# A hybrid encoder layer in fp32: moving weight splits, residual loads, token operands and one POOL subtraction

## The chip, the cores and the metric

The kernel runs on one core of a Trainium2 chip, in one launch. The metric is device time in microseconds, the median of several runs; lower is better. The engines are named as in the profile: PE (TensorE, matmuls), PEld (its weight loads), DVE (VectorE), ACT (ScalarE), POOL (GpSimd) and SP (SyncE, here a queue of DMAs).

## The reference

One encoder layer over two sequences, 2048 tokens (sample) and 256 tokens (prompt), with 1024 channels and shared weights:

```
p = rmsnorm(x) @ W_in                       # 2336 columns
a = bidirectional gated linear attention    # 4 heads, 512 channels, chunks of 64
b = spatial gating over chunks of 128       # 256 channels
c = centred mean pooling, windows 2/4/8/16  # 256 channels
x = x + concat(a, b, c) @ W_o
h = rmsnorm(x)
gate, up = split(h @ W1)                    # 2 x 2816 columns
x = x + (silu(conv3(gate)) * up) @ W2       # depthwise conv of width 3 over tokens
y = rmsnorm(x)
```

All is in fp32. Each large product is made of three fp32r matmuls: both operands are split into a high and a low part (hi = the rounded copy, lo = source - hi), and hi*hi + hi*lo + lo*hi is added up in PSUM.

## The kernel before, in words

**Splits and ticks.** `split` (L159) makes the high part on ACT (L161 or, with a scale, L164) and the low part on DVE or POOL (L162, L165). `mm3` (L168) is the three matmuls. Small work that goes along with the matmuls is written as Python generators in a `Pipe` (L91): after each group of three matmuls the program calls `tick`, and every generator that is due issues its next step; what it yields is the number of ticks to its next one. From the second tile of the second sweep on, DVE, ACT, POOL and SP execute in just the order in which the program issues their work (`manual_schedule`, L854); PE does so everywhere. Before that the framework's planner orders DVE, ACT, POOL and SP by its own estimate of when each instruction can start.

**First sweep** (L189 to L494). 18 token tiles of 128. The first 1312 columns of W_in are split once into eight tiles wk; each token tile is multiplied by them (`main1`), 24 ticks a tile, and `post1` does the attention inside the chunks. Masked copies go into buffers af and ab and the low-rank gate into lrs, two of each (NZ). From tile 12 on the raw second weights, wb, are loaded into the ring rawt of four buffers, which `wo_prep` used before. The last tile runs with k outermost, so that the wk tiles come free one after the other; its evictions and its post1 (`end1`) are issued in the second sweep.

**Second sweep** (L497 to L876). The other 1024 columns, wb, are split into eight tiles vk. These lie where wk lay. Three `w2prep(k)` are issued ahead of the first tile's matmuls, the others between them; each asks for the raw tile four further on as it ends. `main2` makes gates and spatial gating, `out2` multiplies by W_o for a group of tiles (SUPERS), adds x, stores the sum to DRAM (d_x) and adds up squares; `stat2` turns these into the norm's factors with a matmul over ones. The last `out2` runs while the FFN's first operands are made (L1360).

**FFN** (L886 to L1405). Three blocks of 2 x 384 tokens (the last with the prompt). h @ W1 is done by Strassen's scheme in its seven-product form: per FFN tile j (22 of them, 128 gate and 128 up columns each) seven products of 4 ticks each, in this order, with token operands in brackets: A11 (B11), S1 (T1), S2 (T2), S3 (T3), S4 (B22), A12 (B21), A22 (T4); 28 ticks in all (`ffn1`). The products go into five PSUM banks fA to fE; A12 adds to fA and A22 to fD, so fD must have been read by `u3` (L1202) first.

The weight operands are made one step a product by `operands` (L1081), four of them ahead in fa. In block 0 each j loads A11, A12, A21, A22 (rawop), makes S1 to S4 on POOL (`comb`, L1072) and stores them to DRAM; the later blocks load all seven. Low halves of A are on DVE, of S on POOL (L1079). The token operands lie in four tiles B0 to B3 by pairs p (B0: B11, B21; B1: T3, B22; B2: T1, T2; B3: T4, half as wide), of one buffer each. For blocks 1 and 2 `bmake` writes them unsplit to DRAM and `bload` (L1031), started with the last FFN tile of the block before, loads and splits the sixteen pieces (four k by four p), with the low halves of p = 0 and 2 on DVE and of p = 1 and 3 on POOL (PAIRS).

After the products of a j, `gate` (L1172) runs twice, for each half of the tokens: conv and SiLU between ACT and DVE, then a split into uh and ul. `ffn2` (L1251) multiplies by W2 after each part of 2 or 3 tiles (PARTS; the FFN always runs one tile ahead) and adds into x2, the residual, loaded by `load2f` (L1275) from d_x. With a block's last part, `sqadd` takes squares on ACT (L1242) and adds them on POOL (L1244), `finish` (L1283) makes the norm's factor, scales x2, stores y and loads the next block's x2. At the very end `last_norm` (L1320) does the same for group 0, with the chain cut short.

The order of SP's queue around the change: at the end of the second sweep the stores of out2, the four transfers of x2 (L924, two for each half), then the stores and loads of `operands` (L1070, L1065).

Of the kernel before, what the change touches and what calls it, by code (L numbers as in the profile page):

```python
# [18 lines left out]
P = 128  # L19
# [21 lines left out]
HW1 = 656  # L41
EV = 0
TX = (4, 0, 3, 1)
# [8 lines left out]
HP = (5, 3, 3, 3)  # L52
HL = (1, 2)
BM = (12, 9, 1, 6, 3)
# [65 lines left out]
def trunk(ctx: ExitStack, tc: tile.TileContext, xT, wa, wb, gw2, gb, rows, wsT, plw, wo, w1, w2, vec, cst, yT):  # L120
# [66 lines left out]
    msk = swp.tile([P, 2, P], U8, name="msk")  # L187
    xpool = pool("xpool", 2)
    if True:  # L189
        w1p = pool("s1w", 1)  # L190
# [67 lines left out]
        SY.dma_start(out=pw, in_=plw)  # L258
        NZ = 2
        af = [sp.tile([P, 512], F32, name=f"af{i}", bufs=1) for i in range(NZ)]  # L260
# [218 lines left out]
        for i in range(NT):  # L479
            if i + 2 < NT:  # L480
                load1(i + 2)
            if 1 <= i < NT - 1:
                next(prep1(i + 1), None)
            if 2 <= i < 2 + KD:
                pipe.add(wo_prep(i - 2), 1)
            if i >= 12 and len(pre) < NRAW:
                k = len(pre)
                pre[k] = rawt("rawb")
                SY.dma_start(out=pre[k], in_=wb[k])
            if i == 0:  # L490
                main1([0, 1])
            elif i > 1:
                end1 = main1([i])
# [3 lines left out]
    if True:  # L497
# [3 lines left out]
        sp2 = s2p  # L501
        wh = [wp.tile([P, 2, W2C], F32R, name=f"vk{k}") for k in range(KD)]
        ws = wp.tile([P, 4, P], F32, name="ws")
# [144 lines left out]
        def main2(i, n, get, t0, more):  # L648
# [11 lines left out]
            if n == 0:  # L660
                for k in range(KD):
                    for g in (1, 0):
                        if g and k + 3 < KD:
                            w2prep(k + 3)
                        mm(k, g)
# [104 lines left out]
        def out2(u, get, between=None, begun=None):  # L770
# [15 lines left out]
            for c in range(KD):  # L786
# [19 lines left out]
                else:  # L806
                    SY.dma_start(out=d_x[u][:, c], in_=xf)
                    for _ in sums(c, xf):
                        pass
            pipe.add(stat2(u, acc, alloc), 8)  # L810

# [18 lines left out]

        def wbload(k):
            pre[k] = rawt("rawb")
            SY.dma_start(out=pre[k], in_=wb[k])

        def w2prep(k):
            for cols in ((slice(512, 1024), slice(0, 512)) if k == 0 else (slice(0, 1024),)):
                split(wh[k][:, 0, cols], wh[k][:, 1, cols], pre[k][:, cols], vc[:, V_G1 + k:V_G1 + k + 1])
            if k + NRAW < KD:
                wbload(k + NRAW)

        for _ in load2(seq[0][1]):
            pass
        for k in range(3):
            w2prep(k)
            if k == EV:
                end1()
# [30 lines left out]
        s2p.release()  # L877
        w2p.release()
        xpool.release()
        swp.release()  # L880
# [5 lines left out]
    if True:  # L886
# [57 lines left out]
        BP = dict(B11=(0, 0), B21=(0, 1), T3=(1, 0), B22=(1, 1), T1=(2, 0), T2=(2, 1), T4=(3, 0))  # L944
        PAIRS = ((0, V), (2, V), (1, GP), (3, GP))

# [84 lines left out]
        def bload(bi, box):  # L1031
# [8 lines left out]

            for p, _ in PAIRS:
                load(0, p)
            yield box["wait"]
            for kk in range(4):
                for p, eng in PAIRS:
                    m = 2 if p < 3 else 1
                    hi, src = B[p][:, 0, 0:m, kk, 0:w], got.pop((kk, p))
                    SC.activation(hi, src, AF.Copy)
                    yield HL[0]
                    eng.tensor_tensor(out=B[p][:, 1, 0:m, kk, 0:w], in0=src, in1=hi.bitcast(F32), op=ALU.subtract)  # L1050
                    yield HL[1]
                    if kk < 3:
                        load(kk + 1, p)

# [26 lines left out]
        def operands():  # L1081
# [14 lines left out]
            for j in range(NJ):  # L1096
                more = j + 1 < NJ
                operand(j, "A11", a11)
                a12 = rawop(j, "A12")
                s2 = comb(rawt4("S2"), s1, a11, ALU.subtract)  # L1100
                yield
                operand(j, "S1", s1)
                keep(j, "S1", s1)
                s3 = comb(a21, a11, a21, ALU.subtract)
                yield
# [214 lines left out]
        def last_norm(blk, q, xs, no, acc):  # L1320
# [17 lines left out]
            for b, c0 in enumerate(starts):  # L1338
                n = min(P, no - b * P)
                o, i, sc = dg[:, b * P:b * P + n], ident[:, P - n:P], r[:, b:b + 1]  # L1340
                if b % 2:
                    SC.activation(o, i, AF.Copy, scale=sc)
                else:
                    V.tensor_scalar(out=o, in0=i, scalar1=sc, scalar2=None, op0=ALU.mult)
            TE.matmul(pr, ones, dg, start=True, stop=True)
# [17 lines left out]
        fu = pool("fu", 1)  # L1363
        xs = {q: load2f(segs, q, box["w"]) for q, segs in enumerate(BLOCKS[0])}
        for bi, blk in enumerate(BLOCKS):
# [3 lines left out]
            no = box["w"] - 2  # L1369
            nbox = {"wait": 30}  # L1370
            for q, n in enumerate(PARTS):
# [22 lines left out]
            if final:  # L1394
                pipe.flush()
                last_norm(blk, 0, xs, no, accs[0][0])
            else:
                nx = {}
                for q in range(2):
                    def nxt(q=q, nx=nx, segs=BLOCKS[bi + 1][q], w=nbox["w"]):  # L1400
                        nx[q] = load2f(segs, q, w)
                    pipe.add(finish(blk, q, xs, no, accs[q][0], FG, nxt), 2 + 26 * q)
                xs, box = nx, nbox
# [74 lines left out]
```

## Time and profile before

| | us |
|---|---|
| median of 3 runs | 2453.44 (2451.5 to 2454.14) |
| the profiled execution | 2454.75 |
| its span, first to last instruction | 2453.0 |
| PE busy | 2382.1 (97%) |
| PEld busy | 2268.6 (92%) |
| DVE busy | 1679.3 (68%) |
| ACT busy | 1034.4 (42%) |
| POOL busy | 794.2 (32%) |

The mean granted clock of PE was 0.989 of 2.4 GHz. Busy time counts an engine's work on data; waiting and DMA issue are not in it. Matmuls are pipelined, so a row of a matmul is longer than the distance to the next one. The first sweep lies at 0 to 373 us, the second at 373 to 839, and the three FFN blocks end near 1383, 1913 and 2435.

### The profile page before, as it was taken

The page shows a single profiled execution, that of the slowest core. Times are in us where ns is not written, and L with a number is a line of the kernel's source. Part 1 is how long each engine was busy: PE and PEld are TensorE (multiplying, and loading weights), DVE is VectorE, ACT ScalarE, POOL GpSimd, SP SyncE. Part 2 cuts the span into 40 slices and gives each one's busy share as a digit, 9 for nine tenths or more (in the row PEclk, how much of TensorE's full clock was granted, in tenths as well). Part 3 has the DMA queues.
Part 4 walks back from the last instruction along what each step waited for, and adds up shares of the span by engine and source line. Part 5 has one row for each costly group of instructions (what it writes and reads, how often), then busy time and mean ns, then how long its engine had stood idle before and what let it go on. Part 6 is the DMA issues. An engine that isn't in the chain of part 4 may idle for free.

```text
span 2453.0 us, 36854 instructions
## 1 busy us (share of the span) xinstructions
PE 2382.1 (97%) x13280; PEld 2268.6 (92%) x13280; DVE 1679.3 (68%) x2981; ACT 1034.4 (42%) x1928; POOL 794.2 (32%) x748
## 2 busy tenths in 40 slices
PE   8999998999999889999999899999999999999997
PEld 7899996988988789999999899999999999999997
DVE  6766657676666786777777686666677766666666
ACT  6444445333333443333334544433345533344334
POOL 3332221111011664455444622323223521222122
PEclk9999999999999999999999999999999999999998
DMA  6333224565664754454535464444434543333222
GB/s 202 136 129 112 78 73 150 173 191 149 205 191 128 221 164 128 136 171 155 159 104 160 142 223 118 145 134 126 127 102 155 181 138 100 103 112 104 92 94 87
DMA packets 227771, 343.51 MB, mean 140 GB/s; under 512 B 25634, under 2 KB 124962, under 8 KB 227588
## 3 DMA queue, kind: packets, MB, share of 16 engines
q1 hardware_dynamic: 220564, 318.21, 41.7%
q0 software_dynamic: 6752, 22.55, 2.4%
q8 instruction: 105, 1.72, 0.3%
q14 instruction: 78, 0.64, 0.1%
q10 hardware_dynamic: 272, 0.39, 0.0%
HBM read 261.81 MB, written 79.25 MB: 139 GB/s over the span
## 4 chain that ended last, share of the span: by engine, by line
PE 53%; DVE 4%; issue 3%; POOL 3%; DMA 1%; ACT 1%; SPq 0%; DVEq 0%; POOLq 0%; ACTq 0%
PE py L171 7%; PE py L170 6%; PE py L169 6%; PE fD L1158 3%; PE fA L1160 3%; PE fD L1159 3%; PE fA L1158 3%; PE fD L1160 3%; PE fA L1159 3%; PE fB L1158 2%; PE fB L1160 2%; PE fB L1159 2%; PE fC L1158 2%; PE fC L1160 2%; PE fC L1159 2%
## 5 line engine op out<-in xcount | busy, mean ns | idle before, releaser
L162 POOL TENSOR_TENSOR S<-S,S 128x512 fp32r<-128x512 f32 x242 | 329.7, 1363 | 757.5 <-ACT S L161 724.1
L171 PE MATMUL py<-uh,gl 128*128 128x384 f32 (+1 forms) x1056 | 359.2, 340 | 6.8 <-DVE gl L1225 6.7
L169 PE MATMUL py<-uh,gh 128*128 128x384 f32 (+1 forms) x1056 | 359.6, 341 | 3.2 <-ACT gh L1223 3.1
L170 PE MATMUL py<-ul,gh 128*128 128x384 f32 (+1 forms) x1056 | 358.9, 340 | 3.7 <-DVE ul L1188 3.7
L1270 DVE TENSOR_TENSOR x<-py,x 128x384 f32<-128x384 f32 (+1 forms) x384 | 213.1, 556 | 159.3 <-PE py L171 157.6
L162 DVE TENSOR_TENSOR A<-A,A 128x512 fp32r<-128x512 f32 x198 | 158.0, 798 | 178.5 <-ACT A L161 169.9
L161 ACT ACTIVATE A<-A 128x512 fp32r<-128x512 f32 x198 | 124.4, 630 | 218.8 <-issue 71.0
L171 PEld LDWEIGHTS py<-uh,gl 128*128 128x128 f32 x1056 | 200.1, 190 | 10.4 <-DVE gl L1225 10.4
L161 ACT ACTIVATE S<-S 128x512 fp32r<-128x512 f32 x242 | 152.2, 629 | 135.3 <-PE fE L1160 62.1
L170 PEld LDWEIGHTS py<-ul,gh 128*128 128x128 f32 x1056 | 200.1, 190 | 5.7 <-DVE ul L1188 5.3
L169 PEld LDWEIGHTS py<-uh,gh 128*128 128x128 f32 x1056 | 200.2, 190 | 4.8 <-ACT gh L1223 4.4
L1223 ACT ACTIVATE gh<-rg 128x384 fp32r<-128x384 f32 (+1 forms) x198 | 97.4, 493 | 223.8 <-PE py L170 207.0
L1158 PE MATMUL fA<-B,A 128*128 128x386 f32 (+1 forms) x528 | 180.2, 341 | 0.0
L1160 PE MATMUL fA<-B,A 128*128 128x386 f32 (+1 forms) x528 | 179.3, 339 | 0.0
L1159 PE MATMUL fA<-B,A 128*128 128x386 f32 (+1 forms) x528 | 178.6, 338 | 0.0
L169 PE MATMUL pm<-wk,xh 128*128 128x512 f32 (+2 forms) x432 | 166.4, 385 | 7.0 <-ACT wk L164 6.7
L170 PE MATMUL pm<-wk,xh 128*128 128x512 f32 (+2 forms) x432 | 157.0, 363 | 0.4 <-DVE wk L165 0.3
L171 PE MATMUL pm<-wk,xl 128*128 128x512 f32 (+2 forms) x432 | 156.2, 362 | 0.6 <-DVE xl L162 0.6
L1225 DVE TENSOR_TENSOR gl<-rg,gh 128x384 fp32r<-128x384 f32 (+1 forms) x198 | 119.4, 603 | 8.0 <-ACT gh L1223 8.0
L171 PE MATMUL pw<-mh,ol 128*128 128x512 f32 (+1 forms) x320 | 118.7, 371 | 2.9 <-DVE ol L162 2.9
L169 PE MATMUL qm<-vk,xh 128*128 128x512 f32 x288 | 118.9, 413 | 2.2 <-ACT vk L164 2.2
L169 PE MATMUL pw<-mh,oh 128*128 128x512 f32 (+1 forms) x320 | 118.4, 370 | 0.0
(279 smaller groups left out, 6223.2 us busy)
## 6 DMA issues: line engine op xcount, KB each, us to landing
A<-in_w SPq DMA_DIRECT2D x242, 256.0 KB, 3.7
S<-ds_S SPq DMA_DIRECT2D x176, 256.0 KB, 2.7
rg<-in_w SPq DMA_DIRECT2D x150, 192.0 KB, 2.7
xt<-in_xT SPq DMA_DIRECT2D x35, 512.0 KB, 4.3
ds_S<-S SPq DMA_DIRECT2D x66, 256.0 KB, 2.1
rawo<-dw SPq DMA_DIRECT2D x64, 256.0 KB, 4.4
dx<-xr SPq DMA_DIRECT2D x24, 256.0 KB, 2.5
rg<-in_w SPq DMA_DIRECT2D x48, 128.0 KB, 2.3
```

The source lines that it names most:

```text
L161: SC.activation(hi, src, AF.Copy)
L162: (eng or V).tensor_tensor(out=lo, in0=src, in1=hi.bitcast(F32), op=ALU.subtract)
L169: TE.matmul(out, lh, rhs_h, start=first, stop=False)
L170: TE.matmul(out, lh, rhs_l, start=False, stop=False)
L171: TE.matmul(out, ll, rhs_h, start=False, stop=last)
L1158: TE.matmul(o, ah, bh, start=st, stop=False, skip_group_check=True)
L1159: TE.matmul(o, ah, bl, start=False, stop=False, skip_group_check=True)
L1160: TE.matmul(o, al, bh, start=False, stop=kk == 3, skip_group_check=True)
L1223: SC.activation(gh[:, 0:n], rv, AF.Copy)
L1225: V.tensor_tensor(out=gl[:, 0:n], in0=rv, in1=gh[:, 0:n].bitcast(F32), op=ALU.subtract)
L1270: V.tensor_tensor(out=x2[:, c, 1:1 + no], in0=py[q][:, 0:no], in1=x2[:, c, 1:1 + no], op=ALU.add)
```

## The change

The edits, in the order of the program:

- **Second weights.** A new pool vx holds vk0 and vk1 (NVX = 2), apart from the others, so that they do not lie on wk. `w2early` runs `w2prep(0)` and `w2prep(1)` 12 ticks after tiles 15 and 16 of the first sweep begin, and each asks for a raw tile four further on. The second sweep begins with `w2prep` of 2, 3 and 4. The first split is no longer halved. NZ is 1 instead of 2.
- **stat2** of the last out2 is added 16 instead of 8 ticks on.
- **bload** takes its sixteen pieces at the ticks of a table, BORDER, counted from the start of the block's last FFN tile: the four of p = 2 at 13 to 22, p = 0 and 1 at 42 to 68, p = 3 at 78 to 90. `nbox["wait"]` (30) is gone.
- **S3** is subtracted one step earlier, straight behind S2.
- **last_norm**: the four diagonal pieces are all on ACT, and the pipe is flushed behind them instead of ahead of last_norm.
- **First residual**: the two `load2f` of block 0 are put off by XG = 30 and 60 ticks.
- **finish** of a block's two halves is added at 14 and 36 ticks instead of 2 and 28.

```diff
-EV = 0
+NVX = 2
-HL = (1, 2)
+XG = 30
+BORDER = ((0, 2, 13), (1, 2, 16), (2, 2, 19), (3, 2, 22), (0, 0, 42), (0, 1, 45), (1, 0, 48), (1, 1, 52),
+          (2, 0, 56), (2, 1, 60), (3, 0, 64), (3, 1, 68), (0, 3, 78), (1, 3, 82), (2, 3, 86), (3, 3, 90))
...
+    vx = pool("vx", 1)
+    vk = [vx.tile([P, 2, W2C], F32R, name=f"vk{k}") for k in range(NVX)]
...
+    def w2prep(k):
+        split(vk[k][:, 0], vk[k][:, 1], pre[k], vc[:, V_G1 + k:V_G1 + k + 1])
+        if k + NRAW < KD:
+            wbload(k + NRAW)
+
+    def w2early(k):
+        w2prep(k)
+        return
+        yield
...
-        NZ = 2
+        NZ = 1
...
+            if NT - 1 - NVX <= i < NT - 1:
+                pipe.add(w2early(i - NT + 1 + NVX), 12)
...
-                        if g and k + 3 < KD:
-                            w2prep(k + 3)
+                        if g and k + NVX + 3 < KD:
+                            w2prep(k + NVX + 3)
...
-            pipe.add(stat2(u, acc, alloc), 8)
+            pipe.add(stat2(u, acc, alloc), 16 if between else 8)
...
-        for k in range(3):
+        for k in range(NVX, NVX + 3):
             w2prep(k)
-            if k == EV:
+            if k == NVX:
                 end1()
...
-            for p, _ in PAIRS:
-                load(0, p)
-            yield box["wait"]
-            for kk in range(4):
-                for p, eng in PAIRS:
-                    m = 2 if p < 3 else 1
-                    hi, src = B[p][:, 0, 0:m, kk, 0:w], got.pop((kk, p))
-                    SC.activation(hi, src, AF.Copy)
-                    yield HL[0]
-                    eng.tensor_tensor(out=B[p][:, 1, 0:m, kk, 0:w], in0=src, in1=hi.bitcast(F32), op=ALU.subtract)
-                    yield HL[1]
-                    if kk < 3:
-                        load(kk + 1, p)
+            todo = [(kk, p) for kk, p, _ in BORDER]
+            for kk, p in todo[:NX - 1]:
+                load(kk, p)
+            at = 0
+            for n, (kk, p, tick) in enumerate(BORDER):
+                if tick > at:
+                    yield tick - at
+                    at = tick
+                m = 2 if p < 3 else 1
+                hi, src = B[p][:, 0, 0:m, kk, 0:w], got.pop((kk, p))
+                SC.activation(hi, src, AF.Copy)
+                yield 1
+                (GP if p % 2 else V).tensor_tensor(out=B[p][:, 1, 0:m, kk, 0:w], in0=src, in1=hi.bitcast(F32), op=ALU.subtract)
+                yield 1
+                at += 2
+                if n + NX - 1 < len(todo):
+                    load(*todo[n + NX - 1])
...
                 s2 = comb(rawt4("S2"), s1, a11, ALU.subtract)
+                s3 = comb(a21, a11, a21, ALU.subtract)
                 yield
                 operand(j, "S1", s1)
                 keep(j, "S1", s1)
-                s3 = comb(a21, a11, a21, ALU.subtract)
...
-                o, i, sc = dg[:, b * P:b * P + n], ident[:, P - n:P], r[:, b:b + 1]
-                if b % 2:
-                    SC.activation(o, i, AF.Copy, scale=sc)
-                else:
-                    V.tensor_scalar(out=o, in0=i, scalar1=sc, scalar2=None, op0=ALU.mult)
+                SC.activation(dg[:, b * P:b * P + n], ident[:, P - n:P], AF.Copy, scale=r[:, b:b + 1])
+            pipe.flush()
             TE.matmul(pr, ones, dg, start=True, stop=True)
...
-        xs = {q: load2f(segs, q, box["w"]) for q, segs in enumerate(BLOCKS[0])}
+        xs = {}
+
+        def first_x(w):
+            for q, segs in enumerate(BLOCKS[0]):
+                xs[q] = load2f(segs, q, w)
+                yield XG
+
+        pipe.add(first_x(box["w"]), XG)
...
             if final:
-                pipe.flush()
                 last_norm(blk, 0, xs, no, accs[0][0])
...
-                    pipe.add(finish(blk, q, xs, no, accs[q][0], FG, nxt), 2 + 26 * q)
+                    pipe.add(finish(blk, q, xs, no, accs[q][0], FG, nxt), 14 + 22 * q)
```

## Rows read from the trace of the kernel before

**Rows 1.** The page's head and its part 1: busy us (share) xinstructions.

```profile
span 2453.0 us, 36854 instructions
...
PE 2382.1 (97%) x13280; PEld 2268.6 (92%) x13280; DVE 1679.3 (68%) x2981; ACT 1034.4 (42%) x1928; POOL 794.2 (32%) x748
```

**Rows 2.** PE's waits, whole run: us in total, times, longest us.

```profile
PE fD L1158 <- DVE u L1167: 10.4, 3, 8.4
...
PE py L170 <- DVE ul L1188: 3.7, 3, 2.0
...
PE pn L705 <- DVE acc L784: 1.8, 1, 1.8
```

**Rows 3.** Windows at half clock: length, then PE, PEld, DVE, ACT, POOL busy, PEclk, DMA.

```profile
390.80:394.20 3.40, 3.40 (x12) 3.08 (x13) 3.30 (x10) 2.59 (x4) 0.00 (x0) 0.50 0.04 13
858.40:868.60 10.20, 5.25 (x16) 5.28 (x17) 4.88 (x6) 4.47 (x6) 5.79 (x4) 0.50 0.57 198
...
sum 17.00, PE 16.02 PEld 15.52 DVE 5.99 ACT 5.42 POOL 12.45; mean PE 5.34 PEld 5.17 DVE 2.00 ACT 1.81 POOL 4.15
```

**Rows 4.** PE's waits from 372 to 392 us, second sweep's start.

```profile
PE qm L170 <- DVE vk L165: 2.4, 4, 0.8
PE qm L169 <- ACT vk L164: 2.2, 3, 1.1
```

**Rows 5.** Groups by form, 372 to 392: vk's low halves, busy us, mean ns, idle before.

```profile
L165 DVE SCALAR_TENSOR_TENSOR vk<-rawb,vc,vk 128x1024 fp32r<-128x1024 f32 x7 | 8.8, 1281 | 3.6 <-ACT vk L164 3.6
```

**Rows 6.** Window from 392 to 420, columns as in rows 3.

```profile
392.00:420.00 28.00, 22.66 (x123) 18.28 (x123) 23.39 (x72) 10.52 (x16) 5.89 (x8) 0.93 0.28 94
```

**Rows 7.** Window at the first sweep's end, tiles 15 and 16, columns as before.

```profile
320.00:360.00 40.00, 39.67 (x248) 35.57 (x247) 25.08 (x53) 18.56 (x35) 9.29 (x18) 1.00 0.22 79
```

**Rows 8.** DMA issues from 844 to 864: KB each, median us to landing.

```profile
x<-dx SPq DMA_DIRECT2D x1, 1540.0 KB, 10.3
...
A<-in_w SPq DMA_DIRECT2D x5, 256.0 KB, 9.2
```

**Rows 9.** The page's part 6, DMA issues of the whole run.

```profile
A<-in_w SPq DMA_DIRECT2D x242, 256.0 KB, 3.7
```

**Rows 10.** Timeline of SP, block 1's first x2 load: start us, us.

```profile
1419.74 1.24 SPq L924 DMA_DIRECT2D x<-dx  x2
```

**Rows 11.** PE's waits from 1357 to 1920 us: all groups of them.

```profile
PE pn L1290 <- POOL acc L1244: 5.7, 2, 4.3
PE py L169 <- ACT gh L1223: 2.1, 1, 2.1
PE py L171 <- DVE gl L1225: 1.8, 3, 1.1
PE py L170 <- DVE ul L1188: 1.4, 1, 1.4
```

**Rows 12.** POOL's groups by form, 1356 to 1394: busy us, mean ns, idle before.

```profile
L1244 POOL TENSOR_TENSOR acc<-acc,sq 128x384 f32<-128x384 f32 x14 | 18.5, 1340 | 0.0
L1050 POOL TENSOR_TENSOR B<-b,B 128x772 fp32r<-128x772 f32 x4 | 8.8, 2190 | 5.8 <-ACT B L1048 5.8
```

**Rows 13.** Window over block 0's last gates, columns as in rows 3.

```profile
1343.70:1356.00 12.30, 10.36 (x60) 10.05 (x58) 10.21 (x18) 6.16 (x13) 2.59 (x2) 1.00 0.83 305
```

**Rows 14.** DVE's wide low halves: one in the timeline, the group from 1359 to 1384.

```profile
1356.85 0.96 DVE L1050 TENSOR_TENSOR B<-b,B 128x772 fp32r<-128x772 f32 x1 [0.18 <-ACT B L1048]
...
L1050 DVE TENSOR_TENSOR B<-b,B 128x772 fp32r<-128x772 f32 x7 | 9.1, 1305 | 0.0
```

**Rows 15.** Timelines of POOL and PE: S1's low half, and PE's first use.

```profile
894.75 1.73 POOL L162 TENSOR_TENSOR S<-S,S 128x512 fp32r<-128x512 f32 x1
...
900.32 0.35 PE L1158 MATMUL fC<-B,S 128*128 128x386 f32 x1
```

**Rows 16.** Timelines of ACT, DVE and POOL at the end.

```profile
2430.61 1.16 ACT L1299 ACTIVATE acc<-ident,rt 128x128 f32<-128x128 f32 x4
2436.14 3.27 DVE L1307 SCALAR_TENSOR_TENSOR x<-x,vc,acc 128x386 f32<-128x386 f32 x6
2439.83 1.01 POOL L1337 TENSOR_TENSOR rt<-rt,mhalf 128x4 f32<-128x4 f32 x1 [9.97 <-DVE rt L1336]
```

More of the change, by code (lines that the diff above doesn't have):

```diff
@@ L188, in trunk, with wbload @@
     xpool = pool("xpool", 2)
+    vx = pool("vx", 1)
+    vk = [vx.tile([P, 2, W2C], F32R, name=f"vk{k}") for k in range(NVX)]
+    def wbload(k):
+        pre[k] = rawt("rawb")
+        SY.dma_start(out=pre[k], in_=wb[k])
+    def w2prep(k):
[6 more added lines that the diff above has]
+        yield
     if True:
@@ L486, in trunk @@
             if i >= 12 and len(pre) < NRAW:
-                k = len(pre)
-                pre[k] = rawt("rawb")
-                SY.dma_start(out=pre[k], in_=wb[k])
+                wbload(len(pre))
+            if NT - 1 - NVX <= i < NT - 1:
+                pipe.add(w2early(i - NT + 1 + NVX), 12)
             if i == 0:
@@ L501, in trunk @@
         sp2 = s2p
-        wh = [wp.tile([P, 2, W2C], F32R, name=f"vk{k}") for k in range(KD)]
+        vk += [wp.tile([P, 2, W2C], F32R, name=f"vk{k}") for k in range(NVX, KD)]
+        wh = vk
         ws = wp.tile([P, 4, P], F32, name="ws")
@@ L829, in trunk @@
         seq = [(u, t) for u, ts in enumerate(tiles_of) for runs in (SUPERS[u],) for t in order_of(runs)]
[L831 to L839, printed above, removed]
         for _ in load2(seq[0][1]):
             pass
-        for k in range(3):
+        for k in range(NVX, NVX + 3):
             w2prep(k)
-            if k == EV:
+            if k == NVX:
                 end1()
@@ L878, in trunk @@
         w2p.release()
+        vx.release()
         xpool.release()
@@ L944, in trunk @@
         BP = dict(B11=(0, 0), B21=(0, 1), T3=(1, 0), B22=(1, 1), T1=(2, 0), T2=(2, 1), T4=(3, 0))
-        PAIRS = ((0, V), (2, V), (1, GP), (3, GP))
         def btiles():
@@ L1369, in trunk @@
             no = box["w"] - 2
-            nbox = {"wait": 30}
+            nbox = {}
             for q, n in enumerate(PARTS):
```

## The prediction

> **What bounds the kernel now.** The page's first part comes first: TensorE (PE) is busy 2382.1 us of a span of 2453.0 [rows 1], so about 71 us without a matmul are all that can be won, and the question at each edit is which wait of PE it touches. 2382.1 us for 13280 matmuls is 0.18 us each, or 0.54 us for a tick of the planner, which is three matmuls. The view of PE's waits then says who ends them [rows 2]: the longest single one, 8.4 us, is product fD waiting for DVE's u3; 3.7 us in three waits are for ul, the low half of a gate's output; 1.8 us are for out2's last sum of squares. Third come the stretches in which the granted clock reads 0.50, 1.2 instead of 2.4 GHz [rows 3]. Each begins at or just behind one of PE's longer idle times, and what PE did in it took twice as long, so each costs half of PE's busy time in it: 5.25 / 2 = 2.6 us behind the 8.4 us wait, 3.40 / 2 = 1.7 us at 390.8. So a long stall is paid about one and a third times. Last come the timelines of the stages that the change touches, stage by stage below.
>
> **The change part by part**, against the profiled execution's own 2454.75 us (span 2453.0 and 1.75 around it). The median of the three runs, 2453.44, is 1.3 lower.
>
> *A. Two of w_B's eight splits go into the first sweep.* At the start of the second sweep PE waits 2.4 us for DVE's and 2.2 us for ACT's vk [rows 4], 4.6 in all, and 1.7 more follow at half clock at 390.8. With vk0 and vk1 made earlier, PE has four of the sixteen groups of its first tile before it needs vk2, and the raw loads of k = 4 and 5 have gone too, so those of 6 and 7 are asked for straight behind vk2 and vk3. Six splits of 1.28 us on DVE remain [rows 5], at the pace of PE's own groups; I let 1.3 us of the 6.3 stay: -5.0. The next stretch is another matter: from 392 to 420 DVE is busy 23.39 of 28 us and PE 22.66 [rows 6]; its idle 5.3 us come from post1's chain for tile 17 on a loaded DVE, which PE will only reach sooner. I leave them. Bounds: 0 (the stall moves whole into that chain) to -11.6 (6.3 and 5.3).
> The moved work costs 2 x 1.28 us of DVE and about as much of ACT inside tiles 15 and 16, and two 512 KB loads on SP's queue behind all x loads but the second sweep's. Before the sweep's end PE works 39.67 of 40 us with DVE at 25.08 and ACT at 18.56 [rows 7]; that idle time hides it: 0. Uncovered it costs 2.6. NVX also takes away the halved first split and one copy of af, ab and lrs (NZ 1): the next tile writes them some 24 ticks later on the same DVE, or after PE has long read lrs: 0, and three fills fewer on POOL at the start, which PE does not wait for.
>
> *B. The residual loads wait 30 and 60 ticks.* Now four transfers, 3.1 MB, enter SP's queue just ahead of the weights of the first FFN tiles. The large ones land after 10.3 us and the five weight loads behind them after 9.2 [rows 8], where 3.7 is the median of all 242 [rows 9]. ACT's split of A22 waits for its load, DVE's u3 is queued behind that split, and PE stands 8.4 us. With the loads put off, A22 has none of these 3.1 MB in front of it and is needed at the same tick: -8.4 and -2.6 of half clock = -11.0. What is late next: u3 itself, which by its chain of two additions and a split comes out about level with PE. The two loads then fall behind the first weights of tiles 1 and 2, one x tile at a time, and PE first needs x after four FFN tiles, 112 ticks. In the later blocks the same kind of tile is loaded at 1419.74 among weights and operands [rows 10], and of PE's waits from 1357 to 1920 none is for either [rows 11]. Those blocks have their raw operands asked for further ahead, so a part can come back: bounds 0 to -13.
>
> *C1. stat2 sixteen ticks after instead of eight*: the 1.8 us wait [rows 2] is PE reaching its sums before DVE has added the last square. Eight ticks are 4.3 us, so it goes; u3 then has 1.8 us less, of which I count 0.3: -1.5 (0 to -1.8).
>
> *C2. Token operands (bload) in the order of BORDER.* This happens twice, at the end of blocks 0 and 1. Now all sixteen pieces follow 30 ticks after the last FFN tile begins, three ticks apart, behind the gates and through the whole of ffn2. There POOL does fourteen additions of squares, 18.5 us, and four wide low halves, 8.8 us [rows 12], besides four narrow ones of half that width, and the additions follow each other without idle time. Between 1357 and 1920 PE waits 5.7 us for POOL's acc, 2.1 for gh (ACT held by the squares' buffers, which POOL frees) and 1.8 for gl [rows 11]: 9.6 us. The half clock behind the acc and gh waits is worth 16.02 / 2 = 8.0 us (the sum row of [rows 3]). After the change the narrow pieces lie in the next FFN tile, four of DVE's eight wide pieces have left ffn2, and finish reads acc 12 and 8 ticks later, 4.3 us or more. SP asks for three pieces ahead instead of four, over the same four buffers. POOL's load in ffn2 falls by the narrow pieces, so it lags by half: the 17.6 us go.
> What takes their place: four wide splits (p = 2) now run at ticks 13 to 24 of the last FFN tile, on DVE ahead of the gates' own instructions. DVE is busy 10.21 of the 12.30 us up to the gates' end [rows 13], 2.1 idle. Four wide low halves take 0.96 us each where POOL is still and 1.305 in the mean beside it [rows 14], 3.84 to 5.22 us. So ul, for which PE waits already (2.0 us at the first place, part of the 3.7 in rows 2), comes 1.7 to 3.1 us later if all idle time is used; the gates' turns between ACT and DVE keep some of it from being used. I take 2.2 at the first place and 1.5 at the second, where DVE has more room, and 3.1 for both in half clock, as in the stretches of rows 3: 6.8 back. Sum -17.6 + 6.8 = -10.8. Bounds: -22 (ul's own waits vanish too, with what follows them) to +2 (POOL still late at one of the two places, ul 5 us later at each).
> The Trainium skill has a rule that speaks against these early pieces: by SBUF — State Buffer, Who interferes with whom, a DVE instruction with two inputs in SBUF contends with a GpSimd instruction that reads SBUF, and whoever starts second waits for the whole of the other. The trace agrees in kind: 0.96 us alone, 1.305 beside POOL. POOL works 2.59 us in that window, so by the rule up to 2.6 us per place come on top, and the sum would end 5 us higher.
>
> *D. S3 beside S2.* No instruction is added; on POOL the subtraction for S3 now precedes the low half of S1. That half starts at 894.75 and takes 1.73 us, and PE reads it at 900.32 [rows 15], 3.8 us later. Delayed by a subtraction of the same shape, some 1.7 us, it is still in time: 0. Bounds: 0, or the stall of rival 4.
>
> *E. The last norm.* Today finish's six remaining multiplications (3.27 us of DVE) stand in front of last_norm's two small DVE operations, and POOL's power waits till 2439.83 [rows 16]. Moved behind the diagonal they run beside POOL, ACT and PE. The power can come between 0 and 3.27 us earlier; PE's own last sums lie in that time too, and I take the middle, 1.7. Four diagonal pieces on ACT took 1.16 us [rows 16], against half of it shared with DVE: -1.7 + 0.6 = -1.1. The stores of group 1 end later and meet the last ones for a moment: -1.0. Bounds: +0.6 (only the diagonal is longer) to -3.3.
>
> **Sum**: -5.0 - 11.0 - 1.5 - 10.8 - 1.0 = -29.3, so 2425.4 for an execution like the profiled one, 2424 as a median of runs.
>
> **Rivals.**
> 1. *The gates eat the gain of C2.* The early splits push ul by their full price at both places, and POOL's squares are still late once. For it: DVE is busy 83% of that window already. Against it: finish has 4.3 us more or better. C2 counts 0: 2435.
> 2. *Everything clears.* DVE fits the early pieces into its idle time, and the second sweep's chain for tile 17 moves up with its splits: 6.8 + 5.3 more, 2412. Against it: DVE's busy share in both windows.
> 3. *The put-off x loads block again.* Each is 1.5 MB ahead of the next A11; two waits of about 5 us bring the 11 back: 2435. Against it: the stretch behind 1419.74.
> 4. *The other side: S1 becomes the late operand.* The S3 subtraction ahead of S1's low half costs nothing while 3.8 us of slack hold. Where POOL lags by more than 2.1 us, PE waits for it, in each of block 0's 22 FFN tiles: at most 22 x 1.73 = 38 us, 2424 + 38 = 2462, slower. Against it: POOL has time to catch up in every ffn2, where no operand is made.
> 5. *It doesn't do what it says.* vk0 and vk1 are queued behind the sweep's last evictions by the planner, and the x loads block: without A and B some 2440; with C2 at 0 as well, 2451, no change.
>
> **How the numbers follow.** Forecast 0.50, rival 1 0.18, rival 2 0.15, rival 3 0.08, rival 4 0.05, rival 5 at its no-change end 0.04. Time 2424. The range runs from rival 2 to a little beyond rivals 1 and 3, 2412 to 2440; the forecast's own is 2418 to 2431. Within 0.2%, 4.9 us, is what a measurement here can't tell from no change: faster 0.91, same 0.05 (rival 5, and a mild form of 4), slower 0.04.
>
> **What would show it.** After: fD's wait for u under 1 us in the first FFN tile, weights there landing in about 4 us, and no clock of 0.50 around 858; no wait of pn for acc in either ffn2's wake; the wait for ul at both block ends longer than before, 3 to 4 us; vk's waits around 373 to 391 down to some 1 us; S waits of PE none. A long wait of fB or fC for POOL's S in block 0 would mean rival 4; a wait for A with x loads in flight, rival 3. Shorter waits for ul would prove my price of the early splits wrong. An unchanged total with these waits gone would mean that they had only moved.

## Result and the profile after

The changed kernel takes 2436.18 us (median of 6 runs, 2432.92 to 2438.52), the kernel before 2453.02 in the same comparison: a ratio of 0.9933, 95% interval 0.992 to 0.9946. That is 16.8 us less, faster as forecast and inside the range, but 12 us short of the 2424. The profiled execution took 2438.52.

The page's head and first part:

```profile
span 2436.8 us, 36852 instructions
PE 2376.9 (98%) x13280; PEld 2265.2 (93%) x13280; DVE 1671.8 (69%) x2978; ACT 1036.7 (43%) x1929; POOL 795.5 (33%) x745
```

Against [rows 1] PE is 5.2 us less busy, and its idle time falls from 70.9 to 59.9 us. The view of PE's waits of the whole run, beside [rows 2]:

```profile
PE py L173 <- DVE gl L1239: 7.3, 9, 1.4
...
PE fD L1172 <- DVE u L1181: 6.0, 5, 1.9
PE py L172 <- DVE ul L1202: 4.4, 3, 2.1
...
PE pz L359 <- DVE lrs L352: 2.1, 2, 1.5
```

The 8.4 us wait and pn's waits for POOL's acc are gone. But fD still waits 6.0 us for u, now five times, and gl and ul cost no less than before. Stage by stage, from the starts of the same matmuls in both timelines (us):

| stretch | before | after | change | forecast |
|---|---|---|---|---|
| start to the fifth token tile | 90.18 | 94.10 | +3.9 | 0 |
| rest of the first sweep | 283.46 | 282.44 | -1.0 | 0 |
| second sweep, first two tiles | 40.88 | 38.37 | -2.5 | -5.0 (A) |
| rest of the second sweep | 424.74 | 423.76 | -1.0 | 0 |
| first FFN tile | 28.09 | 16.51 | -11.6 | -12.5 (B, C1) |
| up to the fifth FFN tile | 74.31 | 76.99 | +2.7 | 0 |
| up to block 0's last FFN tile | 395.17 | 391.03 | -4.1 | 0 (D) |
| from there to block 1's fifth | 140.48 | 137.80 | -2.7 | -5.4 (C2) |
| the same, block 1 to 2 | 138.51 | 138.69 | +0.2 | -5.4 (C2) |
| middles of blocks 1 and 2 | 776.25 | 776.87 | +0.6 | 0 |
| last FFN tile to the end | 60.90 | 60.18 | -0.7 | -1.0 (E) |

So the total lies inside the range by luck: block 0's middle won what no step had promised, and the two block ends won 2.5 us where 10.8 were forecast. Without the step that won it (D, experiment 1) the changed kernel takes 2445.8, outside 2412 to 2440.

Of the 2.7 us lost up to the fifth FFN tile, 1.7 are a half clock of 3.4 us at 903.4, behind a 1.81 us wait of fD for u. The kernel before has the same wait (1.79) and no half clock behind it.

### The profile page after: what moved, and what is told of

It is laid out like the page before. It is cut to its first block, busy times and chain, and to the rows that moved or that the text cites. A ratio compares the mean times of both kernels' runs of the same rounds, so it can differ in the third digit from the quotient of the medians.

```text
span 2436.8 us, 36852 instructions
## 1 busy us (share of the span) xinstructions
PE 2376.9 (98%) x13280; PEld 2265.2 (93%) x13280; DVE 1671.8 (69%) x2978; ACT 1036.7 (43%) x1929; POOL 795.5 (33%) x745
## 4 chain that ended last, share of the span: by engine, by line
PE 52%; DVE 4%; issue 4%; POOL 3%; DMA 2%; ACT 1%; SPq 0%; DVEq 0%; POOLq 0%; ACTq 0%
PE py L173 7%; PE py L172 7%; PE py L171 6%; PE fA L1174 3%; PE fA L1172 3%; PE fA L1173 3%; PE fD L1172 3%; PE fD L1173 3%; PE fD L1174 3%; PE fC L1174 2%; PE fC L1172 2%; PE fC L1173 2%; PE fB L1174 2%; PE fB L1173 2%; PE fB L1172 2%
## 5 line engine op out<-in xcount | busy, mean ns | idle before, releaser
L1239 DVE TENSOR_TENSOR gl<-rg,gh 128x384 fp32r<-128x384 f32 (+1 forms) x198 | 125.8, 635 | 9.2 <-ACT gh L1237 9.2
L172 PE MATMUL pw<-ml,oh 128*128 128x512 f32 (+1 forms) x320 | 118.3, 370 | 0.1
```

Of the source, the lines that this page charges most:

```text
L172: TE.matmul(out, lh, rhs_l, start=False, stop=False)
L1239: V.tensor_tensor(out=gl[:, 0:n], in0=rv, in1=gh[:, 0:n].bitcast(F32), op=ALU.subtract)
```

## Experiments

Lengths of stretches below are those of the table's rows, from each run's own timeline. The kernel before ran beside each group and took 2452.1 to 2453.7.

**1. D taken back in the changed kernel.**

```diff
                 s2 = comb(rawt4("S2"), s1, a11, ALU.subtract)
-                s3 = comb(a21, a11, a21, ALU.subtract)
                 yield
                 operand(j, "S1", s1)
                 keep(j, "S1", s1)
+                s3 = comb(a21, a11, a21, ALU.subtract)
```

> The changed kernel with S3's subtraction back behind S1's split; nothing else. My theory (D is worth nothing, and the 4.1 us that block 0 gains between its fifth and its last FFN tile come from elsewhere): the run takes the changed kernel's time, within 1 us, and the stretch from the fifth to the 22nd FFN tile of block 0 keeps its length. Rival (moving S3 is what shortened gl's waits there): that stretch is some 4 us longer, and the run about 2440. The first sweep is the same program as in the changed kernel: if its 3.9 us of loss against the kernel before are fixed by the program, they stand here too; if they are one execution's chance, the half clock near 74 us is absent in some of these runs.

2445.82 us: the rival held for the stretch, and the run is slower than its 2440. Block 0's middle is 394.96 long (391.03 with D), the stretch in front of it 79.08 (76.99), the rest of the second sweep 1.8 longer (0.7 of it at 664 us, ahead of D's first instruction at 797, so not by D). The timelines of POOL and DVE around one gate, first with D taken back, then in the changed kernel:

```profile
1119.02 1.60 POOL L1087 TENSOR_TENSOR A<-A,A 128x512 f32<-128x512 f32 x1
...
1119.40 1.63 DVE L1191 SCALAR_TENSOR_TENSOR t<-e,vc,t 128x384 f32<-128x384 f32 x1
...
1120.58 1.61 POOL L164 TENSOR_TENSOR S<-S,S 128x512 fp32r<-128x512 f32 x1
...
1121.07 1.53 DVE L1192 SCALAR_TENSOR_TENSOR t<-e,vc,t 128x384 f32<-128x384 f32 x1
```

```profile
1116.35 0.61 DVE L1191 SCALAR_TENSOR_TENSOR t<-e,vc,t 128x384 f32<-128x384 f32 x1
...
1116.67 1.43 POOL L164 TENSOR_TENSOR S<-S,S 128x512 fp32r<-128x512 f32 x1 [0.67 <-ACT S L163]
...
1116.99 1.53 DVE L1192 SCALAR_TENSOR_TENSOR t<-e,vc,t 128x384 f32<-128x384 f32 x1
```

Each of these two multiplications of a gate reads both inputs from SBUF. One takes 0.61 us alone and 1.5 to 1.6 when a POOL instruction runs beside it: it ends some 0.4 us after POOL's. With the subtraction late, two POOL instructions in a row lie beside the gate and stretch both multiplications; with it early, one does. The Trainium skill's rule (SBUF — State Buffer, Who interferes with whom: of a DVE instruction with two SBUF inputs and a GpSimd one that reads SBUF, the later starter waits for all of the other) agrees with these rows.

**2. D alone in the kernel before.** The diff of experiment 1 the other way round.

> The kernel before with D alone: S3's subtraction in front of S1's split. The run with D taken back said that D is worth some 7 us in the changed kernel, against the 0 of my prediction. Theory now (D is worth that by itself, through the gates: S4's low half on POOL ends earlier and no longer lies beside both of a gate's multiplications on DVE): about 2446, with some 3.5 to 4 us of it between the fifth and the 22nd FFN tile of block 0. Rival (D pays only once B has made the first tiles come earlier, and in the kernel before its cover is still there): 2452, within 1 us of the kernel before.

2448.11 beside 2453.74, so the theory held. Its span is 6.7 less than that of the kernel before's profiled execution, 4.3 of it in block 0's middle (390.87 for 395.17). The groups of DVE in that stretch, before and with D alone (mean ns behind the busy time):

```profile
L1178 DVE SCALAR_TENSOR_TENSOR t<-e,vc,t 128x384 f32<-128x384 f32 x17 | 26.0, 1527 | 0.6
...
L1177 DVE SCALAR_TENSOR_TENSOR t<-e,vc,t 128x384 f32<-128x384 f32 x17 | 21.6, 1269 | 8.6 <-ACT t L1175 8.6
L1178 DVE SCALAR_TENSOR_TENSOR t<-fA,vc,t 128x384 f32<-128x384 f32 x16 | 9.9, 618 | 0.6
```

```profile
L1178 DVE SCALAR_TENSOR_TENSOR t<-e,vc,t 128x384 f32<-128x384 f32 x17 | 16.0, 940 | 0.6
...
L1177 DVE SCALAR_TENSOR_TENSOR t<-e,vc,t 128x384 f32<-128x384 f32 x17 | 15.3, 902 | 8.6 <-ACT t L1175 8.6
```

The pair falls from 2.80 to 1.84 us, and what is queued behind it comes earlier: PE's waits for gl and gh there fall from 4.9 to 2.2 us, its idle time from 5.11 to 2.16 (windows of 395.17 and 390.87 with PE busy 390.06 and 388.71). The other 1.35 us are PE busy time; the clock is 1.00 in both windows, and their cause stays open. The line with fA is a control: the same operation in the gate of the other half of the tokens reads one input from PSUM, and POOL does not stretch it.

**3. B undone.**

```diff
-        pipe.add(first_x(box["w"]), XG)
+        for q, segs in enumerate(BLOCKS[0]):
+            xs[q] = load2f(segs, q, box["w"])
```

> The changed kernel with B undone: both residual loads at once. By my prediction 11.0 us come back (the wait of fD for u of some 8 us in the first FFN tile and a half clock of some 5 us length behind it): 2447. Rival (D, which makes S2 and S3 earlier, or C1 did part of it): the wait is shorter, 2 to 5 us, and the run takes 2439 to 2443.

2446.62. The first FFN tile takes 27.48 us (16.51). PE's waits there, and the landing times of weights issued among the x loads:

```profile
PE fD L1172 <- DVE u L1181: 8.5, 2, 8.3
```

```profile
x<-dx SPq DMA_DIRECT2D x1, 1540.0 KB, 10.2
...
A<-in_w SPq DMA_DIRECT2D x5, 256.0 KB, 8.3
```

11.0 us at the place, as forecast; 1.5 of it come back in the next three tiles, where POOL's operands are then in time. The 8.3 us wait stands as it did in [rows 2] although D is in place: D had no part in it.

**4. A undone.**

```diff
-NVX = 2
+NVX = 0
```

> The changed kernel with A undone: no split of w_B in the first sweep, all eight at the start of the second. By my prediction A is worth 5.0 us: 2441, with waits for vk of 4 to 5 us in the second sweep's first tile. By the account of the two traces it gave 4.1 there, so 2440. Rival (the waits behind the first tile, for pz, ptq and pg, only take the place of those for vk): the first tile is longer, the second shorter by as much, and the run stays within 1.5 us of the changed kernel's.

2437.37. The second sweep's first two tiles take 39.95 us instead of 38.37, and the end of the first sweep 1.5 more; vk's waits are 3.4 us in all:

```profile
PE qm L171 <- ACT vk L166: 1.8, 2, 1.3
PE qm L172 <- DVE vk L167: 1.6, 2, 0.8
```

A is worth 3.1 us by its places. The single total moves less, because this execution's start was 4.0 us shorter than that of the changed kernel (see below).

**5. C1 and E undone.**

```diff
-            pipe.add(stat2(u, acc, alloc), 16 if between else 8)
+            pipe.add(stat2(u, acc, alloc), 8)
...
-                SC.activation(dg[:, b * P:b * P + n], ident[:, P - n:P], AF.Copy, scale=r[:, b:b + 1])
-            pipe.flush()
+                if b % 2:
+                    SC.activation(o, i, AF.Copy, scale=sc)
+                else:
+                    V.tensor_scalar(out=o, in0=i, scalar1=sc, scalar2=None, op0=ALU.mult)
...
             if final:
+                pipe.flush()
                 last_norm(blk, 0, xs, no, accs[0][0])
```

> The changed kernel with C1 and E undone, two edits whose stages lie 1600 us apart, read at their own places. By my prediction C1 is worth 1.5 us and E 1.0: 1.5 us more between the last pw and the second FFN tile, with pn's wait for acc of 1.8 us back, and 1.0 more in the tail, 2438.7 in all. Rival for C1 (u3, which is then the next late one, takes its place, or the first FFN tile's S waits do): less than 0.5 us there. Rival for E (the sum of squares of the last output ends last either way): less than 0.3 us.

2437.03. E is worth 0.8 at its place (60.95 for 60.18). Nine of the ten profiled executions with E take 60.1 to 60.4 there and the three without it some 60.9, but one with E also takes 60.9.

Without C1 the first FFN tile is 2.1 longer and the next three 1.8 shorter: 0.2 net. In the first tile pn's wait for acc is back at 1.08 us, with a half clock of 3.4 us behind it. The 1.8 has three parts: waits of 0.63 us for S and 0.20 for u, which only the kernel with C1 has, its half clock behind u's 1.81 us wait (1.7), and on the other side a wait for gl of 0.82, which only the run without C1 has. That run also waits 1.80 for u, with no half clock. So C1's net worth hangs on two half clocks of 1.7 us each, one on either side, and is not shown.

**6. C2 undone.**

```diff
-            todo = [(kk, p) for kk, p, _ in BORDER]
...
+            for p, _ in PAIRS:
+                load(0, p)
+            yield box["wait"]
...
-                    pipe.add(finish(blk, q, xs, no, accs[q][0], FG, nxt), 14 + 22 * q)
+                    pipe.add(finish(blk, q, xs, no, accs[q][0], FG, nxt), 2 + 26 * q)
```

> The changed kernel with C2 undone: the token operands' pieces in their old order and at their old ticks, and the norm behind each block at its old delays. By my prediction C2 was worth 10.8 us, so the run takes 2447. By the account of the two traces the two block ends and the three FFN tiles behind them gave only some 2.5 us together, so 2438 to 2439, with pn's waits for acc (some 4 and 1.5 us) and their half clock back and the 1.5 and 1.9 us waits of fD for u in the fourth FFN tile gone.

2435.60, no slower. The two places take 138.00 and 139.11 us, with C2 137.80 and 138.69: C2 is worth 0.6 us. PE's waits at the first place, without and with it:

```profile
PE py L172 <- ACT gh L1236: 2.1, 1, 2.1
PE py L173 <- DVE ul L1201: 1.4, 1, 1.4
PE pn L1303 <- POOL acc L1257: 1.3, 1, 1.3
PE py L174 <- DVE gl L1238: 0.4, 1, 0.4
```

```profile
PE py L173 <- DVE gl L1239: 2.6, 3, 1.4
PE py L172 <- DVE ul L1202: 2.1, 1, 2.1
PE fD L1172 <- DVE u L1181: 1.5, 1, 1.5
PE py L171 <- ACT uh L1200: 0.7, 1, 0.7
PE py L171 <- ACT gh L1237: 0.5, 1, 0.5
```

The waits for acc and most of gh's went. Longer waits for ul and gl and a new one for u, in the fourth FFN tile of the next block, took their place. The next five runs take these apart.

**7. The second residual load later.**

```diff
-                yield 8
+                yield 8 if q == 0 else 26
                 nxt()
```

> The changed kernel with one edit: the residual load of the second group (1.5 MB in two transfers) is issued 18 ticks later, behind the first w2 loads of that tile instead of just ahead of them. My theory: the new waits of fD for u in the fourth FFN tile of blocks 1 and 2 (1.50 and 1.94 us) come from SP's queue: the w2 pieces are queued behind that load, the split gh waits 4.4 us for them on ACT, gl waits on DVE, and u is queued behind gl. Then both waits go and the run is 3 to 4.5 us faster, 2432 to 2433. Rival (the waits come from the norm's scalings, which now lie beside the gates on DVE): both waits stay, and the time is the same within 1 us.

2431.72; the places take 136.14 and 135.24 us, and the waits for u are gone. The timeline of SP, ACT, DVE and PE around the fourth FFN tile, in the changed kernel and then here:

```profile
1422.52 1.24 SPq L935 DMA_DIRECT2D x<-dx  x2
...
1425.03 0.92 SPq L1230 DMA_DIRECT2D rg<-in_w  x2
...
1431.32 0.52 ACT L1237 ACTIVATE gh<-rg 128x384 fp32r<-128x384 f32 x1 [4.43 <-DMA rg<-in_w]
1431.87 0.56 DVE L1239 TENSOR_TENSOR gl<-rg,gh 128x384 fp32r<-128x384 f32 x1 [2.39 <-ACT gh L1237]
...
1432.35 0.55 DVE L1181 TENSOR_TENSOR u<-fD,e 128x386 f32<-128x386 f32 x1
...
1433.05 0.41 PE L1172 MATMUL fD<-B,A 128*128 128x386 f32 x1 [1.50 <-DVE u L1181]
```

```profile
1419.07 1.02 SPq L1230 DMA_DIRECT2D rg<-in_w  x2
...
1425.10 0.51 ACT L1237 ACTIVATE gh<-rg 128x384 fp32r<-128x384 f32 x1
...
1426.07 1.24 SPq L935 DMA_DIRECT2D x<-dx  x2
...
1428.19 0.55 DVE L1181 TENSOR_TENSOR u<-fD,e 128x386 f32<-128x386 f32 x1
```

The first of these is the chain of B once more, in small. Without C2 too, the 1.5 MB load stands ahead of the w2 pieces (rg) on SP, 4.3 us ahead in the run b_back. ACT's split waits for them there, but PE does not wait for u:

```profile
ACT gh L1236 <- DMA rg<-in_w: 2.8, 1, 2.8
```

C2 put finish 8 ticks later. The load then came 2.5 us ahead of the pieces, ACT's split stood 4.43 us for the first of them, and u queued behind gl on DVE. Counted from the start of the same FFN tile, that piece is issued 4.2 us later than in x_later and lands after 6.3 us instead of 4.6; SP itself stood 2.4 us at the load, until a store of y had landed. Of the 5.1 us won, 1.7 are a half clock of 3.4 us that stood at 1869.4 in the changed kernel, behind ul's 2.07 us wait, and is absent here although that wait is the same. So 3.4 are the load's.

**8. Two of the four early pieces later** (with 7).

```diff
-BORDER = ((0, 2, 13), (1, 2, 16), (2, 2, 19), (3, 2, 22), (0, 0, 42),
+BORDER = ((0, 2, 13), (1, 2, 16), (2, 2, 33), (3, 2, 37), (0, 0, 42),
```

> The later residual load of the run x_later and one edit more: the last two of the four early p = 2 pieces go from ticks 19 and 22, ahead of the gates, to ticks 33 and 37, behind them. My theory: only these two cost anything (in x_later they took DVE 2.00 and 0.96 us in the middle of the gates' chain, the first two lay in idle time), and with them gone uh and ul come as in the run b_back: one wait of 1.41 us in place of 0.66 and 2.06, and no half clock behind it. That is 3.0 us at a place with the half clock and 1.3 at one without: x_later's 2431.7 becomes 2426 to 2429. Rival (the two pieces only move the wait: in the projection DVE is then late with gl, as it was in the kernel before): the waits for gh and gl there, 2.6 us in x_later, double, and the time stays at 2430 to 2433.

2429.05 (4 runs, 2427.29 to 2430.36; ratio to the kernel before 0.99, 0.9885 to 0.9915). The places take 133.66 and 134.06. DVE's pieces in the run x_later, from the timeline:

```profile
1333.38 1.29 POOL L164 TENSOR_TENSOR S<-S,S 128x512 fp32r<-128x512 f32 x1 [6.30 <-DMA A<-in_w]
...
1333.50 2.00 DVE L1063 TENSOR_TENSOR B<-b,B 128x772 fp32r<-128x772 f32 x1
...
1337.07 0.96 DVE L1063 TENSOR_TENSOR B<-b,B 128x772 fp32r<-128x772 f32 x1
...
1341.16 1.23 DVE L1202 TENSOR_TENSOR ul<-t,uh 128x384 fp32r<-128x384 f32 x2
```

These two stood in the gates' way, the first at double price beside a POOL instruction. PE's waits at the first place are now:

```profile
PE py L172 <- DVE gl L1238: 2.7, 3, 1.4
PE py L171 <- DVE ul L1201: 1.8, 1, 1.8
PE py L170 <- ACT gh L1236: 0.5, 1, 0.5
```

ul costs 1.8 for 2.7 (with uh), without a half clock behind it, still 0.4 more than the 1.4 of b_back; gl and gh stay. The gain is 2.5 and 1.2 us, the theory's.

**9. p = 2 on POOL, p = 1 on DVE** (with 7).

```diff
-                (GP if p % 2 else V).tensor_tensor(out=B[p][:, 1, 0:m, kk, 0:w], in0=src, in1=hi.bitcast(F32), op=ALU.subtract)
+                (GP if p > 1 else V).tensor_tensor(out=B[p][:, 1, 0:m, kk, 0:w], in0=src, in1=hi.bitcast(F32), op=ALU.subtract)
```

> The changed kernel with the later residual load of the run x_later and one edit more: POOL makes the low halves of p = 2 (in the last FFN tile of a block) and DVE those of p = 1 (in the last projection), where it was the other way round. My theory: the waits that are left at a block's end come from these two: DVE's early pieces stand in front of the gates (waits for uh and ul of 0.66 and 2.06 us, then 3.4 us at half clock, 1.7 lost), and POOL's pieces hold up the sums of squares and so gh and gl (0.5, 0.76 and 1.37 us). Then 5 to 7 us go at each of the two places: 2431.7 becomes 2418 to 2422. Rival (it is the two engines' common work that counts: POOL's early pieces stretch the gates' own instructions, and DVE's pieces delay the sums in the projection): the waits change name and keep their size, 2430 to 2433.

2437.63, 5.9 more than x_later: my theory failed, and the rival's price was too low. From the timeline:

```profile
1335.13 4.28 POOL L1063 TENSOR_TENSOR B<-b,B 128x772 fp32r<-128x772 f32 x2
...
1335.51 2.21 DVE L1191 SCALAR_TENSOR_TENSOR t<-e,vc,t 128x384 f32<-128x384 f32 x1
...
1337.76 2.07 DVE L1192 SCALAR_TENSOR_TENSOR t<-e,vc,t 128x384 f32<-128x384 f32 x1
```

Both multiplications of the gate run at POOL's pace, and PE waits 3.6 us for uh and 1.8 for ul. It is D's mechanism again: work moved to POOL does not leave DVE alone. In the projection, where POOL now makes no wide piece, gh is in time, but PE still waits 2.1 us for gl, as in x_later.

**10. p = 1 in the next FFN tile** (without 7).

```diff
-          (0, 0, 42), (0, 1, 45), (1, 0, 48), (1, 1, 52), (2, 0, 56), (2, 1, 60), (3, 0, 64), (3, 1, 68),
-          (0, 3, 78), (1, 3, 82), (2, 3, 86), (3, 3, 90))
+          (0, 0, 42), (1, 0, 48), (2, 0, 56), (3, 0, 64), (0, 1, 70), (1, 1, 74), (2, 1, 78), (3, 1, 82),
+          (0, 3, 85), (1, 3, 88), (2, 3, 91), (3, 3, 94))
```

> The changed kernel with one edit: the four wide pieces of the token operand whose low halves POOL makes (p = 1) leave the last projection of a block for its end and the next FFN tile, ticks 70 to 84 instead of 45 to 70. My theory: the waits for gh and gl that are left in that projection (0.49, 0.76 and 1.37 us at the first place) come from POOL, whose wide halves hold up the sums of squares and through their buffers ACT's gh; they go, 2.6 us at each place, 5 in all: about 2431. Rival (they come from DVE's own wide halves): they stay, and T3, read from tick 88, becomes a new wait, so the same time or up to 4 us more.

2446.80. The waits for gh and gl in the projection did go, and the next block's first tile begins 3.2 us sooner. But that tile then stands for POOL's pieces, with 10.2 us at half clock behind it:

```profile
PE fD L1172 <- POOL B L1062: 4.9, 2, 3.6
```

So the p = 1 pieces do hold up gh and gl, and there is no room for all four behind the projection: theory right that the waits go with these pieces, rival on the price, and more of it than it said. For gh the way through POOL stands in ACT's timeline of the changed kernel, where a square waits for POOL's sum and gh is queued behind it:

```profile
1361.40 0.53 ACT L1256 ACTIVATE sq<-x 128x384 f32<-128x384 f32 x1 [2.57 <-POOL acc L1258]
1361.83 0.51 ACT L1237 ACTIVATE gh<-rg 128x384 fp32r<-128x384 f32 x1
```

For gl POOL's wide pieces are not shown to be the cause: in experiment 9 it waits without them.

**11. POOL's pieces first** (with 8).

```diff
-          (2, 2, 33), (3, 2, 37), (0, 0, 42), (0, 1, 45), (1, 0, 48), (1, 1, 52),
-          (2, 0, 56), (2, 1, 60), (3, 0, 64), (3, 1, 68),
+          (0, 1, 31), (2, 2, 34), (1, 1, 37), (3, 2, 40), (2, 1, 43), (0, 0, 46),
+          (3, 1, 49), (1, 0, 52), (2, 0, 57), (3, 0, 62),
```

> As two_later, and POOL's four p = 1 pieces go ahead of DVE's p = 0 pieces, to ticks 31 to 49, where POOL stood still for 7.6 us in x_later. My theory: POOL is then done with its wide pieces when most of the additions of squares come, the squares' buffers come free in time, and the waits for gh and gl (0.5, 0.76 and 1.37 us at each place) go: 4 to 5 us less than two_later, 2422 to 2425. Rival (the early stretch is no free room: loads of the pieces come no faster, and ACT, which makes the high halves in order, stands on them with gh behind): the same time as two_later or up to 4 us more.

2427.39 (4 runs, 2426.67 to 2429.0; 0.9896, 0.9879 to 0.9912). The wait for gh went, gl's two stayed (0.84 and 1.36), and at both places a half clock of 3.4 us came back behind ul's same 1.81 us wait. DVE's timeline ahead of the second wait for gl:

```profile
1353.19 1.24 DVE L1062 TENSOR_TENSOR B<-b,B 128x772 fp32r<-128x772 f32 x1 [1.34 <-ACT B L1060]
1354.35 1.34 DVE L1238 TENSOR_TENSOR gl<-rg,gh 128x384 fp32r<-128x384 f32 x1
```

POOL's last wide piece ends at 1352.6. DVE's own wide piece stands in front of gl and waits for its high half from ACT, and gl, 0.55 us alone, takes 1.34 beside POOL's sums. By the stretches (134.46, 134.95) it is no better than 8; its lower median is not shown to be the edit's. Both runs beat the changed kernel by 7 us or more.

## Why the prediction came out so

**C2 is the step that failed**: "Sum -17.6 + 6.8 = -10.8" is 0.6 when it is undone. *The relief* was sized as if all waits of the projection went. In the run with both side costs removed, two_later, the places are together 9.4 us shorter than without C2, not 17.6. The waits for acc (5.6 us) and the half clocks at the two places went. The waits for gh and gl in the projections, 5.4 us without C2, stand at 5.2: taking narrow pieces from POOL and wide ones from DVE did not bring these in time. ul's waits are 0.8 longer. *The early pieces* cost 3.7 (x_later to two_later), or 5.4 with the half clock at 1869.4 that x_later lacks by chance, less than the 6.8 that I took. *What I left out* is the third term, 5.1, or 3.4 without that half clock: I wrote of finish only that it reads acc later, and did not follow the load that it issues at its end, though [rows 10] show the first of these loads and the text asks for every DMA of a moved step. Rival 1's 2435 came out, but not by its mechanism: PE waits for POOL's acc at neither place, and D's gain is in the total.

**D** failed by "0. Bounds: 0, or the stall". It is worth 6.7 alone, and this unforeseen gain, not the reasoning, kept the time in the range. I looked for the subtraction's reader on PE and never asked which DVE instructions run beside it, and I set no bound below nothing. The price was in reach: the same operation, at 0.61 us alone, had means of 1.27 and 1.53 us in block 0 of the kernel before. Rival 4, POOL late with S1, is there only in small: waits of 0.28, 0.63 and 0.73 us for S in the first three tiles, behind B's gain.

**B** was right in cause and size (11.0 measured). The first weights landed in 5.8 us, not 4, and PE no longer waits for u in the first tile (0.20 in the second). **C1** has the forecast size at its place (2.1 for 1.5), but with a half clock in it, and 0.2 is left after the next tiles. **A** is 3.1 for 5.0: the vk waits went whole, but the wait for lrs comes next, 1.5 us in the same tile, and I had let only 1.3 us of the stall stay. **E** is 0.8 for 1.0.

**The first 90 us** are not shown to have a cause in the change. PE, DVE and ACT execute the same instructions there before and after, and POOL makes three fills fewer. Ten executions whose first sweep is the same program took 90.6 to 94.1 us for this stretch. The six at 92.4 and above have a half clock of 3.4 us near 72 to 77, the four at 91.4 and below have none. The three profiled kernels without the early splits took 90.1 to 90.7, without a half clock; three are too few to call that chance too. The profiled execution was the longest of the ten:

```profile
74.00:77.40 3.40, 3.40 (x16) 3.35 (x15) 1.76 (x5) 1.69 (x3) 1.71 (x3) 0.50 0.67 243
```

Read over one stretch, from the fifth token tile to the end, undoing costs 2.87 us (A), 8.85 (B), 1.17 (C1 and E) and 0.04 (C2), and D alone wins 7.16. That is 20.1 in all, as much as lies between the two profiled executions there. Undoing D in the changed kernel costs 8.55, which makes 21.5. Each figure is a difference of two single executions, in which half clocks of 1.7 us come and go, so that the sum meets so closely is partly luck.

## What to carry to other kernels

When a step is put off, list the DMAs that it issues at its end and see what stands behind them in the queue: 1.5 MB ahead of the next tile's first weights was the same fault in B, where it was cured, and in C2, where it was made worse. When an engine's work is moved, look at what the other engine of the pair is doing at that moment, not only at who reads the result. A step credited with removing several waits should be charged with each instruction that it leaves in the place.

## What the runs showed of the hardware

One wait is not always paid alike. Behind ul's 1.81 us wait the granted clock fell to 0.50 (1.2 of 2.4 GHz) for 3.4 us at both places in pool_first and at neither in two_later; behind the same 2.07 us it fell at the second place in the changed kernel and not in x_later. Each such stretch moves a stage by 1.7 us, and a single profile cannot settle an edit below that.

A gate's multiplication on DVE with both inputs in SBUF (t<-e), 0.61 us alone, took 1.5 to 1.6 beside one POOL instruction of 1.4 to 1.6 us, and 2.1 to 2.2 each beside POOL's wide ones of 2.1. In the kernel before, all 80 of its 132 instructions that took over 0.7 us ended 0.41 to 0.42 us after the POOL instruction beside them. The same operation with one input in PSUM (t<-fA) took 0.60 to 0.62 us all 132 times, 79 of them with more than 0.2 us beside POOL.
